# Loading the factors of both halves of an attention output ahead of its two multiplications

## The chip, the cores and the metric

The kernel runs on one core of one Trainium2 chip. The metric is the device time of one execution in microseconds (us), and a time is the median of several runs. A profile is of one execution; its times count from the start of that execution's span, and its engines are called PE (TensorE matmul), PEld (its weight loads), DVE (VectorE), ACT (ScalarE), POOL (GpSimd) and SP (SyncE, which here issues nearly all DMAs).

## The reference

One layer of a hybrid decoder block on a sequence of 1024 tokens with 1024 features, all in float32. After a conditioned RMSNorm and one input projection it has two branches, a gated DeltaNet (A) and a dilated sliding-window attention in three head groups of four heads (B), which are merged:

```python
o_b = jnp.stack(outs, axis=2)
w_g = jax.nn.softmax(jnp.stack(lses, axis=2), axis=2)
y_b = (o_b * w_g[..., None].astype(o_b.dtype)).reshape(b, s, ATTN_WIDTH) * jax.nn.silu(zb)
y_b = y_b @ w_proj_b[l]

merged = jax.nn.sigmoid(ga) * y_a + jax.nn.sigmoid(gb) * y_b
x = x + gate[:, None] * (merged @ w_out[l])
return rms_norm(x, final_norm_w)
```

The change is about the line with `w_g`: each head's attention output is multiplied by a weight for each token, here called its factor, and then by `silu(zb)`.

## The kernel before

Every tile has 128 partitions. Features lie on the partitions, and the 1024 tokens along the free dimension.

**How the order comes about.** The kernel is written as some hundred generators, called streams (`q_stream`, `ya_split`, `yb_split`, `tail_products` and so on). A planner (`Sched.run`) lets them take turns while the program is being built: it keeps an estimated clock for each engine, resumes the stream with the best priority whose waits have been met by those clocks, and records what the stream issues up to its next `yield`. Each engine then runs its instructions in exactly the recorded order, and waits on semaphores for what the data need. So an instruction that waits holds up everything behind it on its engine. That holds for SP too: a DMA whose target tile is still being read holds up all later DMAs.

Each DMA of SP also signals on one of eight semaphores in turn and waits, before it is issued, for the transfer eight places ahead of it.

**The tail of the program.** From about 1040 us on `tail_products` records, for PE, eight products A (here A product 0 to 7, `pa_units`, 8 x 6 matmuls each, weights `w_pa`), then eight products B (B product 0 to 7, `pb_units`, 6 x 6 matmuls each, weights `w_pb`), then the eight products with `w_out`. A product is a [128, 1024] tile in PSUM; the pool `pj` has two of these. For accuracy each float32 operand is split into a high part (a rounded copy, made by ACT) and a low part (the rest, made by DVE, or by POOL for `w_out`), and `three` records three matmuls for each operand pair, on two halves of 512 columns each: high by high, then high by the factor's low part, then the weights' low part. `YA[0..7]` are the split operands of the A products and `YB[0..5]` those of the B products. Every B product reads `YB[0]` to `YB[5]` in this order, so that B product 0 is the first reader of all six.

An output of an A product (`pa_out`) multiplies it on DVE with a gate tile that was loaded from DRAM (`gate_load`) and frees its place in `pj`; an output of a B product (`pb_out`) does the same, adds the A product's result, and splits the sum for the product with `w_out`.

**The six units.** `YB[j]` is made by `yb_split`, of which two copies run as streams; here its work on one j is called unit j. Unit j holds the two heads `2 * ti` and `2 * ti + 1` of group g (g = j // 2, ti = j % 2). It

1. takes two tiles of the pool `big` and loads the attention output `og` and the gate `z` into them (512 KB each, from `og_d[j]` and `z_d[8 + j]`),
2. multiplies `og` by its factors, 512 tokens at a time. The factors are rows of a small DRAM tensor `fg_d[g]`, written shortly before by `combine(g)`; two DMAs of 128 KB each spread a row over 64 partitions of a tile `fx` of the pool `mid` (six tiles of [128, 512]),
3. multiplies `z` by the result on DVE, with the tokens permuted for g = 1 and 2,
4. splits the product into `YB[j]` (ACT, then DVE).

The pool `big` has 34 tiles. Towards the end of the A products it is full, and the tiles for the last loads are those that A product 7 gives back, one factor of `YA` after another (`big.put(2)` in `tail_products`). The weights of each product come in through the pool `wr` (two tiles), are split into two tiles of `wh`, and the next load into `wr` waits for DVE's half of the split.

All instructions are issued through one helper (`Engine.call`), so the profile gives line 129 to nearly all of them, and one goes by tile names: `og` and `z` are `big`, `fx` is `mid`, `fg_d` is `fgd`, `og_d` is `ogd`, `z_d` is `zd`, and the gates are `gd`.

Of the kernel before, what the change touches and what calls it, by code (L numbers as in the profile page):

```python
# [10 lines left out]
OP = mybir.AluOpType  # L11
# [22 lines left out]
HALVES = (slice(0, 512), slice(512, 1024))  # L34
# [251 lines left out]
def hybrid_block_kernel(ctx: ExitStack, tc: tile.TileContext, x, c, norm_w, ada_w, ada_b, w_tiles, w_vb0, w_vb1,  # L286
# [3 lines left out]
    pe, act, dve, pool, sp = S.pe, S.act, S.dve, S.pool, S.sp  # L290
# [15 lines left out]
    mid = Slots(S, midp, "mid", 6, [P, 512])  # L306
# [624 lines left out]
    def perm(ap, g):  # L931
        if g == 0:
            return ap
        r = 4 if g == 1 else 8
        return ap.rearrange("p (u r) -> p r u", r=r)
# [836 lines left out]
    def split(dst, i, src, ev, slots=None, add=None, owed=0, eng=None):  # L1772
        hi = yield from (slots or big).get(F32R, add=add, owed=owed)
        lo = yield from (slots or big).get(F32R, add=add)
        act.activation(hi, src, AF.Copy)
        yield
        (eng or dve).tensor_tensor(lo, src, hi.bitcast(F32), op=OP.subtract)
        dst[i] = (hi, lo)
        S.set(ev)
# [27 lines left out]
    def yb_split():  # L1807
        yield ev_yas[7]
        while yb_todo:
            j = yb_todo.pop(0)  # L1810
            g, ti = j // 2, j % 2
            rows4 = fg_d[g].rearrange("(h i) p -> h (i p)", h=4)
            yield [ev_fg[g], ev_zd[8 + j]]
            yield lambda: len(big.free_at) > big.debt + 1
            og = yield from big.get()
            z = yield from big.get()
            sp.dma_start(og, og_d[j])
            sp.dma_start(z, z_d[8 + j])
            for q in range(2):
                sl = HALVES[q]  # L1820
                fx = yield from mid.get()
                for hd in range(2):
                    sp.dma_start(fx[64 * hd:64 * hd + 64, :],
                                 rows4[2 * ti + hd:2 * ti + hd + 1, sl].to_broadcast([64, 512]))
                yield
                dve.tensor_tensor(og[:, sl], fx, og[:, sl], op=OP.mult)
                mid.put()
            r = (1, 4, 8)[g]
            dve.tensor_tensor(perm(z, g), perm(z, g), og.rearrange("p (r u) -> p r u", r=r) if g else og, op=OP.mult)
            big.put()  # L1830
            yield
            yield from split(YB, j, z, ev_ybs[j], add=0)
            big.put()
# [217 lines left out]
    S.add(ya_split(), 8, "yas")  # L2051
    S.add(ya_split(), 8.1, "yas")
    S.add(yb_split(), 8, "ybs")
    S.add(yb_split(), 8, "ybs")
    S.add(wo_split(), 8, "wos")
    S.add(rows_stream(), 9, "rows")
# [68 lines left out]
```

## Time and profile before

| | us |
|---|---|
| median of 3 runs | 1280.1 (1279.59 to 1283.01) |
| the profiled execution | 1281.23 |
| its span, first to last instruction | 1279.5 |
| PE busy | 1252.6 |
| DVE busy | 766.2 |
| ACT busy | 502.2 |
| POOL busy | 173.6 |

The DMA engines moved 172.03 MB, 134 GB/s over the span. The mean granted clock of TensorE was 0.996 of full speed. In a timeline a row gives start, duration, engine, operation, the tile written and the tiles read, and in brackets the idle time of the engine ahead of it and what ended that. Busy time of an engine is an average over the span; where the time of a stage goes is read from the waits in that stage.

### The profile page before, as it was taken

Reading aid. Unit: us, or ns where it says so; the run is one execution under the profiler, and the core shown is the slowest. Engines: PE = TensorE matmul, PEld = TensorE weight load, DVE = VectorE, ACT = ScalarE, POOL = GpSimd, SP = SyncE. Lnnn points to the kernel's source line nnn. Section 1 sums busy time; section 2 is a strip of 40 time slices with the busy share of each in tenths; the row PEclk is TensorE's granted clock in tenths of the full one; section 3 lists DMA queues with packets and bytes.
Section 4 is the critical chain, followed back from the end, with each engine's and each line's share of the span. In section 5 each row is a group of like instructions: output and inputs, shape, how many; then the busy total and the mean of one; then the engine's idle time right before and its main releaser. Section 6 shows DMA issues by size and latency. Waiting matters only on the chain.

```text
span 1279.5 us, 19222 instructions
## 1 busy us (share of the span) xinstructions
PE 1252.6 (98%) x7302; PEld 1029.3 (80%) x7302; DVE 766.2 (60%) x1528; ACT 502.2 (39%) x1081; POOL 173.6 (14%) x128
## 2 busy tenths in 40 slices
PE   7999999999999999999999999999999999999997
PEld 3689888988888978888888888887777678778786
DVE  5845893457874368864669834555555546655533
ACT  5524622346223345233462335335555842122211
POOL 4700300033001022000320002300000000002400
PEclk9999999999999999999999999999999999999999
DMA  9534433153422262332343223635454857843322
GB/s 356 199 111 146 120 92 88 67 155 114 112 75 75 78 203 76 98 107 77 107 118 111 74 76 91 227 136 153 141 155 143 270 166 229 267 135 110 143 95 83
DMA packets 112558, 172.03 MB, mean 134 GB/s; under 512 B 41009, under 2 KB 72913, under 8 KB 112466
## 3 DMA queue, kind: packets, MB, share of 16 engines
q1 hardware_dynamic: 112322, 170.55, 42.5%
q8 instruction: 57, 0.93, 0.3%
q14 instruction: 35, 0.29, 0.1%
q10 hardware_dynamic: 144, 0.26, 0.1%
HBM read 123.40 MB, written 47.37 MB: 133 GB/s over the span
## 4 chain that ended last, share of the span: by engine, by line
PE 80%; DMA 5%; DVE 5%; issue 4%; ACT 3%; POOL 2%; SPq 0%; POOLq 0%; DVEq 0%; ACTq 0%
PE pj L129 60%; PE sb L129 20%; DVE big L129 3%; DMA big<-in_x_dram 2%; ACT big L129 1%; DMA wr<-in_w_out_dram 1%; DMA big<-grow 1%; POOL big L129 1%; POOL wh L129 1%; DVE wh L129 1%; ACT L129 1%; DVE mid L129 1%; ACT wh L129 0%; DMA mid<-yad 0%; SPq L129 0%
## 5 line engine op out<-in xcount | busy, mean ns | idle before, releaser
L129 PE MATMUL pj<-big,wh 128*128 128x512 f32 x3356 | 827.1, 398 | 4.5 <-DVE big L129 2.3
L129 PEld LDWEIGHTS pj<-big,wh 128*128 128x128 f32 x3356 | 616.3, 188 | 135.8 <-issue 8.9
L129 ACT ACTIVATE wh<-wr 128x1024 fp32r<-128x1024 f32 (+3 forms) x99 | 97.4, 984 | 242.3 <-PE pj L129 221.7
L129 DVE TENSOR_TENSOR wh<-wr,wh 128x1024 fp32r<-128x1024 f32 (+3 forms) x96 | 115.4, 1202 | 64.9 <-ACT wh L129 64.5
L129 ACT ACTIVATE big<-big 128x1024 f32<-128x1024 f32 (+2 forms) x77 | 74.1, 969 | 185.8 <-DVE big L129 137.3
L129 PE MATMUL pj<-wh,big 128*128 128x256 f32 (+2 forms) x702 | 110.7, 308 | 0.5 <-POOL wh L129 0.3
L129 PE MATMUL sb<-big,wh 128*128 128x512 f32 x368 | 103.4, 421 | 0.0
L129 PEld LDWEIGHTS pj<-wh,big 128*128 128x128 f32 x702 | 96.2, 189 | 6.5 <-POOL wh L129 0.7
L129 DVE SCALAR_TENSOR_TENSOR big<-pj,cw,big 128x1023 f32<-128x1023 f32 (+2 forms) x72 | 92.1, 1279 | 1.7
L129 PEld LDWEIGHTS sb<-big,wh 128*128 128x128 f32 x368 | 67.2, 190 | 20.6 <-issue 8.1
L129 DVE TENSOR_TENSOR big<-big,big 128x1024 f32<-128x1024 f32 (+4 forms) x44 | 58.1, 1326 | 21.6 <-ACT big L129 19.4
L129 PE MATMUL sb<-sq,big 128*128 128x128 f32 x464 | 67.1, 276 | 3.0 <-ACT sq L129 2.2
L129 PEld LDWEIGHTS sb<-sq,big 128*128 128x128 f32 x464 | 62.6, 191 | 8.9 <-ACT sq L129 3.1
L129 POOL TENSOR_TENSOR wh<-wr,wh 128x1024 fp32r<-128x1024 f32 x3 | 9.1, 3048 | 350.5 <-ACT wh L129 350.5
L129 ACT ACTIVATE big<-sb 128x512 f32<-128x512 f32 (+2 forms) x80 | 40.9, 523 | 35.6 <-PE sb L129 35.5
L129 DVE SCALAR_TENSOR_TENSOR sq<-sq,gsm,sb 128x128 f32<-128x128 f32 x48 | 16.6, 345 | 62.9 <-PE sb L129 61.7
L129 PEld LDWEIGHTS sb<-cst,big 128*128 128x128 f32 x268 | 33.9, 145 | 23.8 <-DVE big L129 8.2
L129 PE MATMUL sb<-cst,big 128*128 128x128 f32 x268 | 44.1, 285 | 7.8 <-DVE rstd L129 4.9
L129 PE MATMUL pj<-big,big 128*128 128x512 f32 x210 | 49.3, 390 | 0.0
L129 ACT ACTIVATE mid<-sb 128x512 f32<-128x512 f32 (+3 forms) x48 | 24.0, 501 | 63.7 <-PE sb L129 63.3
L129 ACT ACTIVATE big<-big,sta 128x128 f32<-128x128 f32 (+1 forms) x96 | 42.2, 442 | 13.0 <-DVE sta L129 12.9
L129 DVE CUSTOM_DVE_ANT_0 big<-sb,cst 128x128 f32<-128x128 f32 (+1 forms) x96 | 28.9, 347 | 29.0 <-PE sb L129 26.2
(140 smaller groups left out, 1282.5 us busy)
## 6 DMA issues: line engine op xcount, KB each, us to landing
wr<-in_w_tiles_dram SPq DMA_DIRECT2D x64, 512.0 KB, 4.2
big<-in_ada_w_dram SPq DMA_DIRECT2D x24, 512.0 KB, 9.0
big<-in_x_dram SPq DMA_DIRECT2D x16, 512.0 KB, 5.5
gd<-big SPq DMA_DIRECT2D x16, 512.0 KB, 2.9
big<-gd SPq DMA_DIRECT2D x16, 512.0 KB, 5.4
big<-grow SPq DMA_DIRECT2D x8, 512.0 KB, 5.7
vtd<-big SPq DMA_DIRECT2D x8, 512.0 KB, 2.6
big<-vtd SPq DMA_DIRECT2D x32, 128.0 KB, 5.0
```

The lines of the kernel that those rows point to most:

```text
L129: r = f(*a, **k)
```

## The change

In `yb_split` the two tiles for the factors are taken together, and all four factor DMAs are issued ahead of the multiplications. Before, each half had its own tile, its two DMAs, a `yield`, its multiplication, and gave its tile back.

```diff
             sp.dma_start(og, og_d[j])
             sp.dma_start(z, z_d[8 + j])
+            fx = yield from mid.many(2)
             for q in range(2):
-                sl = HALVES[q]
-                fx = yield from mid.get()
                 for hd in range(2):
-                    sp.dma_start(fx[64 * hd:64 * hd + 64, :],
-                                 rows4[2 * ti + hd:2 * ti + hd + 1, sl].to_broadcast([64, 512]))
-                yield
-                dve.tensor_tensor(og[:, sl], fx, og[:, sl], op=OP.mult)
-                mid.put()
+                    sp.dma_start(fx[q][64 * hd:64 * hd + 64, :],
+                                 rows4[2 * ti + hd:2 * ti + hd + 1, HALVES[q]].to_broadcast([64, 512]))
+            yield
+            for q in range(2):
+                dve.tensor_tensor(og[:, HALVES[q]], fx[q], og[:, HALVES[q]], op=OP.mult)
+            mid.put(2)
             r = (1, 4, 8)[g]
             dve.tensor_tensor(perm(z, g), perm(z, g), og.rearrange("p (r u) -> p r u", r=r) if g else og, op=OP.mult)
```

`many(n)` waits until n tiles of the pool are free and takes them one after the other. Since the planner now has one turn of these streams fewer between the loads and the product with z, it records other instructions in between. The instructions of PE and of POOL stand as before, apart from the buffers that they use; SP, DVE and ACT have the same instructions in another order within the units' stretch.

On SP, the end of the units' loads stood so before. `ogd4` and `zd12` belong to unit 4, `ogd5` and `zd13` to unit 5, `fgd2` are their factors (x2 is the pair of DMAs of one half); `gd7` is the gate of A product 7, `gd8` that of B product 0, `in_w_pb` the weights of a B product:

```order
L129 DMA big251_9691<-gd7_135 128x1024
L129 DMA big252_9703<-ogd4_190 128x1024
L129 DMA big253_9706<-zd12_172 128x1024
L129 DMA mid152_9709<-fgd2_195 64x512 x2
L129 DMA wr85_9730<-in_w_pb_dram 128x768
L129 DMA big256_9735<-ogd5_191 128x1024
L129 DMA big257_9736<-zd13_173 128x1024
L129 DMA mid153_9739<-fgd2_195 64x512 x2
L129 DMA mid154_9757<-fgd2_195 64x512 x2
L129 DMA big258_9772<-gd8_136 128x1024
L129 DMA mid155_9791<-fgd2_195 64x512 x2
```

Here the second half of unit 4 (`mid154`) comes after all of unit 5's first loads, and the second half of unit 5 (`mid155`) after gate 8. Now, at the same place on SP:

```order
L129 DMA big251_9640<-ogd4_190 128x1024
L129 DMA big252_9641<-zd12_172 128x1024
L129 DMA mid152_9644<-fgd2_195 64x512 x2
L129 DMA mid153_9645<-fgd2_195 64x512 x2
L129 DMA wr84_9668<-in_w_pb_dram 128x768
L129 DMA big255_9714<-gd7_135 128x1024
L129 DMA big256_9723<-ogd5_191 128x1024
L129 DMA big257_9724<-zd13_173 128x1024
L129 DMA mid154_9727<-fgd2_195 64x512 x2
L129 DMA mid155_9728<-fgd2_195 64x512 x2
L129 DMA wr85_9746<-in_w_pb_dram 128x768
L129 DMA big260_9784<-gd8_136 128x1024
```

Unit 4's loads have moved together, ahead of gate 7, and unit 5's ahead of gate 8. In the order before, `zd12` goes into the tile of the low part of `YA[0]`, `ogd5` and `gd8` into later tiles of A product 7's factors; now `gd7` goes into the tile of the low part of `YA[0]`, `ogd5` into that of its high part and `zd13` into that of the low part of `YA[1]`.

On DVE, from the output of A product 7 (the first row, which reads `pj79`) to that of B product 0 (the last, `pj80`), before. Rows that read a `mid` multiply half an attention output by its factors, rows of 128x8x128 are products with z, rows that write a `wh` make the low part of weights, and the other rows with 128x1024 make the low part of a unit:

```order
L129 SCALAR_TENSOR_TENSOR big251_9691<-big251_9691,pj79_9693 128x1024
L129 TENSOR_TENSOR wh193_9776<-wr84_9642,wh192_9775 128x768
L129 TENSOR_TENSOR big256_9735<-mid153_9739,big256_9735 128x512
L129 TENSOR_TENSOR big252_9703<-mid154_9757,big252_9703 128x512
L129 TENSOR_TENSOR big253_9706<-big253_9706,big252_9703 128x8x128
L129 TENSOR_TENSOR big256_9735<-mid155_9791,big256_9735 128x512
L129 TENSOR_TENSOR big257_9736<-big257_9736,big256_9735 128x8x128
L129 TENSOR_TENSOR big260_9813<-big253_9706,big259_9812 128x1024
L129 TENSOR_TENSOR big262_9819<-big257_9736,big261_9818 128x1024
L129 SCALAR_TENSOR_TENSOR big258_9772<-big258_9772,pj80_9774 128x1024
```

The low part of unit 4 (`big260`) stands behind the second half of unit 5 (`mid155`) and its product with z. Now, from the output of A product 6 (the first row, `pj78`) to that of B product 0:

```order
L129 SCALAR_TENSOR_TENSOR big250_9630<-big250_9630,pj78_9632 128x1024
L129 TENSOR_TENSOR big254_9706<-big247_9579,big253_9682 128x1024
L129 TENSOR_TENSOR wh191_9709<-wr83_9592,wh190_9708 128x768
L129 TENSOR_TENSOR big259_9740<-big252_9641,big258_9739 128x1024
L129 TENSOR_TENSOR big256_9723<-mid154_9727,big256_9723 128x512
L129 TENSOR_TENSOR big256_9723<-mid155_9728,big256_9723 128x512
L129 TENSOR_TENSOR big257_9724<-big257_9724,big256_9723 128x8x128
L129 SCALAR_TENSOR_TENSOR big255_9714<-big255_9714,pj79_9716 128x1024
L129 TENSOR_TENSOR wh193_9788<-wr84_9668,wh192_9787 128x768
L129 TENSOR_TENSOR big262_9796<-big257_9724,big261_9795 128x1024
L129 SCALAR_TENSOR_TENSOR big260_9784<-big260_9784,pj80_9786 128x1024
```

The low part of unit 4 (`big259`) has moved ahead of all work on unit 5, and the output of A product 7 (`pj79`) behind unit 5's two multiplications and its product with z.

## The prediction

> **What bounds the kernel now.** I read the page first, then the waits of PE (TensorE), then the timelines of the engines around those waits.
>
> ```profile
> span 1279.5 us, 19222 instructions
> PE 1252.6 (98%) x7302; PEld 1029.3 (80%) x7302; DVE 766.2 (60%) x1528; ACT 502.2 (39%) x1081; POOL 173.6 (14%) x128
> ```
>
> PE is busy for 98% of the span, and the change leaves PE's own instructions and their order as they are. So it can save time only where PE stands still, and cost time only where PE newly stands still. The changed code runs from about 1063 us on. These are PE's waits from 1040 us to the end:
>
> ```profile
> PE pj L129 <- DVE big L129: 2.3, 1, 2.3
> PE pj L129 <- ACT big L129: 1.4, 1, 1.4
> PE pj L129 <- POOL wh L129: 0.3, 1, 0.3
> ```
>
> Three waits in 240 us. PE's timeline says where the first two are (the bracket is the idle time ahead and its releaser):
>
> ```profile
> 1068.37 49.69 PE L129 MATMUL pj<-big,wh 128*128 128x512 f32 x218
> 1119.48 0.73 PE L129 MATMUL pj<-big,wh 128*128 128x512 f32 x2 [1.42 <-ACT big L129]
> 1122.52 61.28 PE L129 MATMUL pj<-big,wh 128*128 128x512 f32 x262 [2.31 <-DVE big L129]
> ```
>
> Both lie in B product 0, the first that reads the factors' result. Now DVE (VectorE) there:
>
> ```profile
> 1102.00 1.25 DVE L129 SCALAR_TENSOR_TENSOR big<-big,pj 128x1024 f32<-128x1024 f32 x1
> ...
> 1107.55 0.69 DVE L129 TENSOR_TENSOR big<-mid,big 128x512 f32<-128x512 f32 x1 [1.16 <-DMA mid<-fgd]
> 1112.66 1.22 DVE L129 SCALAR_TENSOR_TENSOR big<-big,pj 128x1024 f32<-128x1024 f32 x1 [4.42 <-PE pj L129]
> 1113.80 0.95 DVE L129 TENSOR_TENSOR wh<-wr,wh 128x768 fp32r<-128x768 f32 x1
> 1114.66 1.49 DVE L129 TENSOR_TENSOR big<-mid,big 128x512 f32<-128x512 f32 x2
> 1116.19 2.15 DVE L129 TENSOR_TENSOR big<-big,big 128x1024 f32<-128x1024 f32 x1
> 1118.52 0.69 DVE L129 TENSOR_TENSOR big<-mid,big 128x512 f32<-128x512 f32 x1 [0.19 <-DMA mid<-fgd]
> 1119.25 4.43 DVE L129 TENSOR_TENSOR big<-big,big 128x1024 f32<-128x1024 f32 x3
> ...
> 1134.88 1.22 DVE L129 SCALAR_TENSOR_TENSOR big<-big,pj 128x1024 f32<-128x1024 f32 x1 [3.44 <-PE pj L129]
> ...
> 1143.04 1.22 DVE L129 SCALAR_TENSOR_TENSOR big<-big,pj 128x1024 f32<-128x1024 f32 x1 [3.33 <-PE pj L129]
> ```
>
> With the order of DVE's rows in hand this reads so. 1107.55 is unit 4's first half, 1112.66 the output of A product 7 (PE has just begun B product 0), 1114.66 the first half of unit 5 and the second of unit 4, 1116.19 unit 4's product with z. At 1118.52 comes unit 5's second half, held until its factors landed. The three from 1119.25 are unit 5's product with z, then the low part of unit 4, then that of unit 5. **Unit 4's low part thus stands behind unit 5's late factors**, and PE's 2.31 us is the wait for it. The 1.42 us before is the high part of unit 4, which ACT (ScalarE) could start only after 1118.3:
>
> ```profile
> 1118.37 1.06 ACT L129 ACTIVATE big<-big 128x1024 fp32r<-128x1024 f32 x1 [5.27 <-DVE big L129]
> ```
>
> The stop has a tail. In the windows of one us, the column behind POOL is the granted clock:
>
> ```profile
> 1123.00:1124.00 1.00, 1.00 (x5) 0.76 (x4) 0.68 (x1) 0.00 (x0) 0.00 (x0) 0.62 0.00 0
> 1124.00:1125.00 1.00, 1.00 (x4) 0.80 (x3) 0.00 (x0) 0.00 (x0) 0.00 (x0) 0.50 0.00 0
> 1125.00:1126.00 1.00, 1.00 (x4) 0.72 (x3) 0.00 (x0) 0.20 (x1) 0.00 (x0) 0.50 0.00 0
> 1126.00:1127.00 1.00, 1.00 (x5) 0.82 (x4) 0.39 (x1) 0.64 (x1) 0.00 (x0) 0.68 0.00 0
> ```
>
> Missing clock: 0.38 + 0.50 + 0.50 + 0.32 = 1.70 us of PE work. A check without the modelled ends: the outputs at 1112.66, 1134.88 and 1143.04 close A product 7, B product 1 and B product 2. A B product at full pace takes 1143.04 - 1134.88 = 8.16 us, so products 0 and 1 lost 22.22 - 2 x 8.16 = **5.90 us**, against 1.42 + 2.31 + 1.70 = 5.43 from the rows. I take 5.90; the 0.47 between them lies in matmul ends that are only modelled.
>
> **The change part by part.** No instruction is added or removed: 12 multiplications of about 0.69 us, 24 factor loads and the six products with z remain. Only their places move, and with them the waits that they stand behind.
>
> *Unit 4.* Today SP (SyncE, which issues these loads) works through its end in this order:
>
> ```profile
> 1093.02 0.34 SPq L129 DMA_DIRECT2D wr<-in_w_pb_dram  x1
> ...
> 1102.68 0.32 SPq L129 DMA_DIRECT2D big<-zd  x1
> ...
> 1105.29 0.34 SPq L129 DMA_DIRECT2D wr<-in_w_pb_dram  x1
> 1105.73 0.57 SPq L129 DMA_DIRECT2D big<-ogd  x1
> 1106.35 0.43 SPq L129 DMA_DIRECT2D big<-zd  x1
> 1106.83 2.67 SPq L129 DMA_DIRECT2D mid<-fgd  x4
> 1109.60 0.54 SPq L129 DMA_DIRECT2D big<-gd  x1
> 1110.18 1.25 SPq L129 DMA_DIRECT2D mid<-fgd  x2
> ```
>
> 1102.68 is unit 4's z, into a tile that A product 7 has to leave first; 1106.83 holds unit 4's second half, and 1110.18 unit 5's second, behind a gate load. In the changed order all six loads of unit 4 stand ahead of the first load that waits for A product 7, and its z goes into a tile of unit 2. Its last multiplication moves ahead of the output of A product 6 (1102.00), its low part ahead of unit 5's multiplications. PE wants it at 1112.66 + 4 x 1.36 = 1118.1 (1.36 is a sixth of 8.16). The cover is more than 10 us, so both stops at unit 4 go. What is late next is unit 5.
>
> *Unit 5.* Now gate load 7, unit 5's output tile and its z wait for A product 7, for the last reads of the first factor's low part, the first's high part and the second's low part. The first is the very release of 1102.68. The others follow two and six matmuls later, 0.45 and 1.36 us at that pace (36 matmuls in 8.16 us): 1103.1 and 1104.0. The z load takes 0.43 us to issue and each factor load 0.62 (1.25 for two), so the last factor load goes out at 1104.0 + 0.5 + 3 x 0.62 = 1106.4, against 1110.8 now. How long does it take to land? The first row is of the tiles that these eight loads of 1103.0 to 1111.0 fill, the second of all transfers from or to the factor rows, the third of the pair at 1110.18:
>
> ```profile
> DMA to landing us min/median/max: 3.6/6.6/7.7
> DMA to landing us min/median/max: 1.4/6.5/8.4
> mid<-fgd SPq DMA_DIRECT2D x2, 128.0 KB, 7.6
> ```
>
> It lands between 1110.0 (3.6) and 1114.8 (8.4); I take 6.6, so 1113.0, because gate 7, unit 5's tile and its z are in flight ahead of it, as in the rows around 1106. From there DVE has the second multiplication 0.73, the product with z 2.15, the output of A product 7 now behind it 1.14, a weight split 0.86 and the low part 1.14: 6.0 us (start to start from the rows above). Unit 5 is ready at 1119.0, at the ends 1116.0 and 1120.8. PE asks for it in the third matmul of the last sixth of B product 0: 1112.66 + 5 x 1.36 + 0.45 = 1119.9. So **nothing is left of the stop at the value I take, and 0.9 us at the far end**. Below nothing cannot come out, since PE keeps its pace ahead of this.
>
> *Output of A product 7.* It now stands on DVE behind unit 5's multiplications: the added wait. At 1113.0 it starts at 1115.9 in place of 1112.66. Queued behind it are the split of B product 2's weights and unit 5's low part, counted above. PE needs its PSUM tile again for B product 1 at 1112.66 + 8.16 = 1120.8: cover 3.7 us.
>
> *Units 0 to 3* cost nothing: PE runs 49.69 us without a stop beside them, and their results are read only after 1112.66.
>
> *After B product 0* everything hangs on PE. The chain of work that ended last has
>
> ```profile
> 1122.52 44.52 PE pj L129 x188
> 1167.04 0.03 ACTq L129
> ...
> 1201.44 59.69 PE pj L129 x262
> ```
>
> The split of the output weights that ends in the third wait (0.3 us at 1201.44) is started by PE itself at 1167.04. It moves forward with PE and stays as long.
>
> **Sum.** The profiled execution took 1281.23 us (span 1279.5, 1.7 around it): 1281.23 - 5.90 = **1275.3**. It lies 1.1 above the median of the runs, 1280.1; the same saving from the median would give 1274.2. I keep 1275.3, for a reason that is the first rival.
>
> **The rivals.**
>
> *1. The slow clock is not in every execution.* The rows show half clock for some 3.4 us after two stops of 1.42 and 2.31 us with two matmuls between, and none after the 0.28 at 1201. If the median execution had the stops and not the slow clock, the median would lose 5.90 - 1.70 = 4.20: 1280.1 - 4.2 = **1275.9**. For it speaks that the fastest run, 1279.59, lies 1.64 under the profiled one; against it, that no trace shows such a run. [...]
>
> *2. Part of the stop stays.* Unit 5's factors land at 8.4 us or a little more, since two more of them travel together: 0.9 to 2.5 us of wait remain, **1276.2 to 1277.8**. For it: the margin is only 0.9 us, and the landing of 7.6 at 1110.18. Against it: fewer bytes are in flight ahead than then.
>
> *3. The wait only moves.* Unit 5's last factors land after 1117 because the three big loads ahead of them crowd the transfers, as at 1110.18 where each took over 7 us. Then unit 5 is ready after 1123, PE stops for 3 to 4 us, and the slow clock returns: **1279 to 1281**. Against it: the issue lies 4.4 us earlier.
>
> *4. Slower: SP's queue slips.* Each load waits for the one issued eight places ahead, and the store of group 1's factors now stands behind two more pairs of factor loads. That store is slow already:
>
> ```profile
> fgd<-mid SPq DMA_DIRECT2D x3, 16.0 KB, 8.0
> ```
>
> If the delay adds up over units 0 to 4, gate load 7 no longer waits for PE but for SP. It decides only beyond 1102.68 - 1094.2 = 8.5 us of slip, where 1094.2 is the issue of B product 2's weights, just ahead of it (now at 1093.02; its buffer comes free 1.14 us later, by the low part of unit 2 that DVE now does before that split). It costs more than the stop did beyond 8.5 + 0.9 + 5.9 = 15.3 us, one for one: at 20 us, 1281.2 + 4.7 = **1286**. Against it: one more landing of 8.0 us is the most that I can find.
>
> That the change does not do what it says is out: the rows of the order show both factor pairs of each unit together.
>
> **How the numbers follow.** About 0.3%, 3.8 us here, is what a measurement can tell from no change; from 1280.1 the bounds are 1276.3 and 1283.9. Forecast (5.9 saved, 1275.3, own range 1274.2 to 1276.2): 0.50. Rival 1 (1275.9): 0.20. Rival 2: 0.14. Rival 3: 0.10. Rival 4: 0.06. Faster takes the forecast and nearly all of rival 1, 0.68; slower is rival 4, 0.06; the rest, 0.26, is the same. The range 1273.8 to 1278.6 holds the first three cases with half a us for the scatter: 0.82 or so.
>
> **What would show it.** Right: no PE wait on ACT or DVE between 1112 and 1125, a granted clock of 1.00 there, B products 8.16 us apart from the first, SP issuing the last factor load at about 1106.4, unit 5's low part done by 1119.9. If the output of A product 7 starts at 1115 to 1116, the DVE order is as read. Rival 2 shows as one PE wait below 2.5 us in the last sixth of B product 0, rival 3 as one of 3 to 4 us with half clock behind it, rival 4 as gate load 7 issued well after 1103. The prediction is wrong if PE's waits go and the time does not fall by 4 us, or if an A product comes to stop before 1112.

## The result and the profile after

| | before | after |
|---|---|---|
| median | 1283.01 us (13 runs, 1279.59 to 1285.82) | 1276.59 us (13 runs, 1272.92 to 1396.33) |
| ratio | | 0.9947, 95% interval 0.9931 to 0.9962 |

The changed kernel is faster by 0.53%, 6.8 us of 1283.01 (4.9 to 8.9 by the interval). The execution profiled with these runs was a disturbed one (1396.33 us at a granted clock of 0.85): the ratio leaves it out, the medians of the table do not and lie 6.4 us apart, and the profile shown is of the repetition that is told below as e1_after, of an execution that took 1277.98 us.

The head of the changed kernel's page, to be set beside 1279.5 and 1252.6 of before:

```profile
span 1276.2 us, 19231 instructions
PE 1251.3 (98%) x7302; PEld 1028.6 (81%) x7302; DVE 766.5 (60%) x1528; ACT 502.3 (39%) x1081; POOL 173.5 (14%) x128
```

PE has as many matmuls as before, and the nine instructions more (19222 before) are waits on semaphores (four more on SP, six on DVE, one fewer on ACT). PE's waits from 1040 us to the end, of the same kernel, and its timeline from the last A products on:

```profile
PE pj L129 <- POOL wh L129: 0.3, 1, 0.3
```

```profile
1071.03 109.53 PE L129 MATMUL pj<-big,wh 128*128 128x512 f32 x482
```

The waits for DVE and ACT are gone: one row of 482 matmuls runs through all of B product 0, where before had three rows with 1.42 and 2.31 us between them. The third wait, for the output weights, stays at 0.3 us.

Now DVE from the output of A product 6 to that of B product 2:

```profile
1107.69 1.23 DVE L129 SCALAR_TENSOR_TENSOR big<-big,pj 128x1024 f32<-128x1024 f32 x1
...
1114.58 0.69 DVE L129 TENSOR_TENSOR big<-mid,big 128x512 f32<-128x512 f32 x1 [2.53 <-DMA mid<-fgd]
1115.70 0.69 DVE L129 TENSOR_TENSOR big<-mid,big 128x512 f32<-128x512 f32 x1 [0.43 <-DMA mid<-fgd]
1116.43 2.16 DVE L129 TENSOR_TENSOR big<-big,big 128x1024 f32<-128x1024 f32 x1
1118.48 1.21 DVE L129 SCALAR_TENSOR_TENSOR big<-big,pj 128x1024 f32<-128x1024 f32 x1
1119.61 0.95 DVE L129 TENSOR_TENSOR wh<-wr,wh 128x768 fp32r<-128x768 f32 x1
1120.47 1.22 DVE L129 TENSOR_TENSOR big<-big,big 128x1024 fp32r<-128x1024 f32 x1
1123.47 1.22 DVE L129 SCALAR_TENSOR_TENSOR big<-big,pj 128x1024 f32<-128x1024 f32 x1 [1.78 <-PE pj L129]
...
1131.63 1.22 DVE L129 SCALAR_TENSOR_TENSOR big<-big,pj 128x1024 f32<-128x1024 f32 x1 [3.33 <-PE pj L129]
...
1139.79 1.22 DVE L129 SCALAR_TENSOR_TENSOR big<-big,pj 128x1024 f32<-128x1024 f32 x1 [3.33 <-PE pj L129]
```

Only unit 5 is left beside the end of A product 7: 1114.58 and 1115.70 are its two halves, each held for its factors. The output of A product 7 (1118.48) stands behind them, then the split of weights, then unit 5's low part at 1120.47. The outputs of B products 0, 1 and 2 follow at 1123.47, 1131.63 and 1139.79, 8.16 us apart from the first.

**A measure for the stop.** The stretch ahead does not end at the same time in every execution: A product 5's output, the last one ahead of all that moves, starts at 1093.61 here and at 1090.90 in the profile of before. So the stop is measured from that output to the output of B product 2. At PE's full pace these lie 2 x 10.88 + 3 x 8.16 = 46.24 us apart (10.88 is eight sixths of 1.36, an A product). What is over that is called **lost** below. The two kernels in the windows of this stretch, before first and after second; the second figure of a row is PE's busy time and the one ahead of the DMA share the granted clock:

```profile
1090.00:1143.00 53.00, 49.27 (x209) 39.99 (x208) 33.38 (x30) 10.96 (x12) 0.00 (x0) 0.97 0.67 202
```

```profile
1093.00:1140.00 47.00, 47.00 (x209) 38.93 (x208) 30.16 (x28) 11.04 (x12) 0.00 (x0) 1.00 0.70 214
```

As many matmuls, 209, take 53 us with 49.27 busy at a clock of 0.97 before, and 47 us, all of them busy at 1.00, after. By the outputs, before lost 1143.04 - 1090.90 - 46.24 = 5.90 us, and after 1139.79 - 1093.61 - 46.24 = -0.06, that is nothing. What comes behind is as long as it was: from B product 2's output to the span's end 1279.5 - 1143.04 = 136.5 us and 1276.2 - 1139.79 = 136.4.

### The profile page after: what moved, and what is told of

Read it like the earlier page. It is cut to its first block, busy times and chain, and to the rows that moved or that the text cites. A ratio compares the mean times of both kernels' runs of the same rounds, so it can differ in the third digit from the quotient of the medians.

```text
span 1394.6 us, 19231 instructions
## 1 busy us (share of the span) xinstructions
PE 1374.4 (99%) x7302; PEld 1074.6 (77%) x7302; DVE 766.5 (55%) x1528; ACT 502.8 (36%) x1081; POOL 171.1 (12%) x128
## 4 chain that ended last, share of the span: by engine, by line
PE 96%; ACT 2%; issue 1%; DMA 1%; DVE 1%; POOL 0%; SPq 0%; POOLq 0%; DVEq 0%; ACTq 0%
PE pj L129 72%; PE sb L129 23%; ACT big L129 1%; DMA mid<-yad 0%; DVE big L129 0%; ACT wh L129 0%; ACT L129 0%; ACT mid L129 0%; DMA big<-in_c_dram 0%; POOL big L129 0%; DVE sq L129 0%; DVE wh L129 0%; POOL rstd L129 0%; ACT junk L129 0%; ACT pj L129 0%
## 5 line engine op out<-in xcount | busy, mean ns | idle before, releaser
L129 PE MATMUL pj<-big,wh 128*128 128x512 f32 x3356 | 908.4, 426 | 0.0
L129 PEld LDWEIGHTS pj<-big,wh 128*128 128x128 f32 x3356 | 634.5, 194 | 186.5 <-issue 11.1
L129 PE MATMUL pj<-wh,big 128*128 128x256 f32 (+2 forms) x702 | 117.8, 321 | 0.0
L129 PE MATMUL sb<-big,wh 128*128 128x512 f32 x368 | 113.7, 452 | 0.0
L129 PEld LDWEIGHTS pj<-wh,big 128*128 128x128 f32 x702 | 101.5, 197 | 7.7
L129 PE MATMUL sb<-sq,big 128*128 128x128 f32 x464 | 74.8, 299 | 2.6 <-ACT sq L129 2.1
L129 PEld LDWEIGHTS sb<-sq,big 128*128 128x128 f32 x464 | 69.3, 205 | 9.9 <-ACT sq L129 2.9
L129 PE MATMUL pj<-big,big 128*128 128x512 f32 x210 | 54.2, 417 | 0.0
L129 DVE SCALAR_TENSOR_TENSOR big<-sb,s_all,big 128x128 f32<-128x128 f32 x128 | 35.2, 344 | 27.0 <-PE sb L129 20.1
L129 PEld LDWEIGHTS pj<-big,big 128*128 128x128 f32 x210 | 40.3, 192 | 12.4
```

The costliest lines, as they stand in the source:

```text
L129: r = f(*a, **k)
```

## The experiments

The theory is the prediction's: the gain is the time for which PE stands still in B product 0 with the slow clock behind it, and it is set by the moment at which the last multiplication of units 4 and 5 is through on DVE. Three rivals: the loading in pairs gains at every unit; what counts is that the two multiplications stand side by side; or the pair of the one late unit does it. The saving is 1 - ratio, times the median of before in the same rounds. The diffs are against the kernel before, and `...` stands for lines left out.

**e1_after.** The changed kernel again, without an edit.

> The changed kernel as it is, for a profile at the full clock. Theory (the stop): the saving is the stop of B product 0 alone, so PE shows no wait on ACT or DVE over 0.9 us between 1112 and 1125 us, the output of A product 7 starts at 1115 to 1116 us, the last factor load of unit 5 is issued near 1106.4 us, and the time is 5 to 7 us under the kernel before in the same rounds. Rival (clock): the stop is still there with 2 us or more, and the saving comes from stretches of half clock that these executions lack.

Measured: 1278.13 us against 1285.48, ratio 0.9943 (0.9922 to 0.9964), 7.3 us saved; nothing lost, as shown. SP at the place that matters:

```profile
1105.34 0.33 SPq L129 DMA_DIRECT2D big<-gd  x1
1105.79 0.35 SPq L129 DMA_DIRECT2D big<-ogd  x1
1106.69 0.32 SPq L129 DMA_DIRECT2D big<-zd  x1
1107.07 2.37 SPq L129 DMA_DIRECT2D mid<-fgd  x4
1110.95 0.34 SPq L129 DMA_DIRECT2D wr<-in_w_pb_dram  x1
```

Gate 7, unit 5's two tiles and its four factor loads go out together, ahead of the weights (`wr`), which can only go out at 1110.95, when the split of the weights before them on DVE is done (1109.95 + 0.97 = 1110.92).

**e8_before_again.** The kernel before, without an edit, for a second profile of it.

> The kernel before once more, for a second profile. Theory (the stop): the same two PE waits, together 3.5 to 4 us, at the same place. [...] Time equal to the kernel before.

Measured: 1283.73 us against 1284.81, ratio 1.0 (0.9984 to 1.0016). PE and the windows behind its stop:

```profile
1122.05 0.73 PE L129 MATMUL pj<-big,wh 128*128 128x512 f32 x2 [2.15 <-ACT big L129]
1124.98 40.40 PE L129 MATMUL pj<-big,wh 128*128 128x512 f32 x170 [2.20 <-DVE big L129]
```

```profile
1124.00:1125.00 1.00, 0.02 (x1) 0.02 (x1) 1.00 (x2) 0.89 (x1) 0.00 (x0) 0.98 0.00 0
1125.00:1126.00 1.00, 1.00 (x2) 0.81 (x3) 1.00 (x1) 0.00 (x0) 0.00 (x0) 0.50 0.00 0
```

The same two stops and the same half clock behind them, in another execution. Lost: 6.50 us, so the two profiles of before stand at 5.90 and 6.50, mean 6.2.

**e2_units45.** Pairs for units 4 and 5 alone; units 0 to 3 as before.

```diff
+            if j >= 4:
+                fx = yield from mid.many(2)
...
+                for q in range(2):
+                    dve.tensor_tensor(og[:, HALVES[q]], fx[q], og[:, HALVES[q]], op=OP.mult)
+                mid.put(2)
+            else:
...
```

> Both factor loads together for units 4 and 5 only; units 0 to 3 load one half at a time as before. Theory (the stop): only what PE waits for in B product 0 counts. Unit 4's low part is ahead of unit 5 on DVE again, and unit 5's last factor load goes out at about 1108.7 us (1110.8 before), so 0.5 to 1.5 us of the stop stay: 4 to 5.5 us saved. Rival (every unit counts): a third of the units gives a third of the saving, about 2 us.

Measured: 1281.74 us against 1285.48, ratio 0.997 (0.9953 to 0.9988), 3.9 us saved. PE keeps two short stops, and no half clock follows them:

```profile
1122.61 0.73 PE L129 MATMUL pj<-big,wh 128*128 128x512 f32 x2 [1.06 <-ACT big L129]
1123.87 41.33 PE L129 MATMUL pj<-big,wh 128*128 128x512 f32 x181 [0.53 <-DVE big L129]
```

Lost: 2.17. On DVE and SP it shows why unit 5 is late:

```profile
1107.68 0.96 DVE L129 TENSOR_TENSOR wh<-wr,wh 128x768 fp32r<-128x768 f32 x1
```

```profile
1108.67 0.34 SPq L129 DMA_DIRECT2D wr<-in_w_pb_dram  x1
1109.11 0.38 SPq L129 DMA_DIRECT2D big<-ogd  x1
1109.54 0.42 SPq L129 DMA_DIRECT2D big<-zd  x1
1110.13 2.37 SPq L129 DMA_DIRECT2D mid<-fgd  x4
```

The weights stand ahead of unit 5 on SP here. They wait for DVE's split, which ends at 1107.68 + 0.96 = 1108.64, and unit 5's loads, which do not need it, queue behind. In the changed kernel it is the other way round. So the late units' pairs alone do not end the whole stop: that takes the pairs of units 0 to 3 too, and by the rows it is the order which the planner then gives to unit 5.

**e3_units0to3.** The counterpart: pairs for units 0 to 3, units 4 and 5 as before.

```diff
+            if j < 4:
+                fx = yield from mid.many(2)
...
```

> Both factor loads together for units 0 to 3 only; units 4 and 5 load one half at a time as before. The planner reaches units 4 and 5 earlier, so that the low part of unit 4 stands ahead of all work on unit 5, and unit 5's last factor load goes out at about 1107 us, ahead of gate 8. Theory (the stop): unit 5 is ready at about 1119.8 us against 1119.9 wanted, so 0 to 1 us of the stop stays: 5 to 6 us saved. Rival (the pairs of units 4 and 5 are what helps): with these loaded one half at a time the stop stays whole, nothing saved. Rival (every unit counts): about 4 us.

Measured: 1281.07 us against 1285.48, ratio 0.9963 (0.9943 to 0.9982), 4.8 us saved. Waits of PE 1.04 and 0.53 us, no half clock, lost 2.09. Units 4 and 5 are loaded one half at a time here, and yet two thirds of the stop are gone. So most of the gain needs no pair at the late unit.

**e9_unit4_only and e10_unit5_only.** A pair for one unit alone (`j == 4`, and `j == 5`).

```diff
+            if j == 4:
+                fx = yield from mid.many(2)
...
```

> Both factor loads together for unit 4 alone. On DVE the low part of unit 4 then stands ahead of unit 5, but on SP the second half of unit 5 now stands behind gate 8 and behind the weights of B product 4, which wait for a split that DVE does after the output of A product 7. Theory (the stop): the stop at unit 4 goes, that at unit 5 grows to 4.5 to 6.5 us in one piece, with half clock behind it: 0 to 4 us slower than the kernel before. Rival (every unit counts): about 1 us saved. Rival (loading a pair together helps the unit that gets it): 2 to 3 us saved, the first of the two stops.

> Both factor loads together for unit 5 alone. On DVE the second half of unit 4 and its product with z now stand behind all of unit 5. Theory (the stop): PE still waits for unit 4, ready at 1122 to 1124 us against 1118.1 wanted (in the times of the profile before), 4 to 6 us of PE waits: from 1.5 us faster to 2 us slower than the kernel before. Rival (every unit counts): about 1 us saved. Rival (unit 5 is the late one, so its pair is the change): 4 to 7 us saved.

Measured, against 1286.57 us: 1287.71, ratio 1.0007 (0.9993 to 1.0021), and 1288.55, ratio 1.001 (0.9993 to 1.0026). Neither gains anything; in the profiles both lose more than before, 7.37 and 8.85 us. PE in the first, then in the second:

```profile
1132.48 32.76 PE L129 MATMUL pj<-big,wh 128*128 128x512 f32 x134 [4.98 <-ACT big L129]
```

```profile
1131.75 33.52 PE L129 MATMUL pj<-big,wh 128*128 128x512 f32 x135 [5.94 <-ACT big L129]
```

The two late places differ. SP in e9_unit4_only, behind unit 5's first pair of factor loads:

```profile
1116.22 1.09 SPq L129 DMA_DIRECT2D mid<-fgd  x2
1117.40 0.53 SPq L129 DMA_DIRECT2D big<-gd  x1
1123.10 0.34 SPq L129 DMA_DIRECT2D wr<-in_w_pb_dram  x1
1123.49 1.09 SPq L129 DMA_DIRECT2D mid<-fgd  x2
```

Unit 5's second half has slipped behind gate 8 and behind one more load of weights, which waits for a split (1122.13 + 0.94 = 1123.07) until 1123.10: 6 us later than it could go. DVE in e10_unit5_only:

```profile
1125.26 0.69 DVE L129 TENSOR_TENSOR big<-mid,big 128x512 f32<-128x512 f32 x1 [0.30 <-DMA mid<-fgd]
1125.99 2.00 DVE L129 TENSOR_TENSOR big<-big,big 128x1024 f32<-128x1024 f32 x1
1127.89 0.68 DVE L129 TENSOR_TENSOR big<-mid,big 128x512 f32<-128x512 f32 x1
```

Here unit 5's pair has overtaken unit 4: the row at 1127.89 is the second half of unit 4, which PE wants first, behind unit 5's second half and its product with z. So a pair is not worth a fixed sum for each unit. What it is worth depends on what it passes.

**e4_loads_together.** The loads of both halves together, but a turn of the planner ahead of each multiplication.

```diff
+            fx = yield from mid.many(2)
...
+            for q in range(2):
                 yield
-                dve.tensor_tensor(og[:, sl], fx, og[:, sl], op=OP.mult)
-                mid.put()
+                dve.tensor_tensor(og[:, HALVES[q]], fx[q], og[:, HALVES[q]], op=OP.mult)
+            mid.put(2)
```

> Both factor loads together in all units, but a turn of the planner ahead of each multiplication. On SP the weights of B product 3 now stand ahead of unit 5's loads, and on DVE the output of A product 7 ahead of unit 5's multiplications. Theory (the stop): unit 5's last factor load goes out at about 1109.7 us, unit 5 is ready at 1121 to 1122, so 1 to 2 us of the stop stay: 3.5 to 5 us saved. Rival (multiplications side by side are what helps): nothing saved, since they are taken one at a time.

Measured: 1279.52 us against 1285.48, ratio 0.9954 (0.9936 to 0.9971), 5.9 us saved. Waits of PE 1.69 and 0.53 us, no half clock, lost 2.74. In e2, e3 and e4 more of the stop stayed than expected: by PE's waits alone 1.59, 1.57 and 2.22 us, against 0.5 to 1.5, 0 to 1 and 1 to 2.

**e5_mults_together.** The counterpart: the multiplications side by side, the second half loaded a turn later than the first.

```diff
+            fx = yield from mid.many(2)
             for q in range(2):
...
+                if q:
+                    yield
                 for hd in range(2):
...
+            yield
+            for q in range(2):
+                dve.tensor_tensor(og[:, HALVES[q]], fx[q], og[:, HALVES[q]], op=OP.mult)
+            mid.put(2)
```

> The two multiplications side by side, but the second half's factors still loaded one turn later than the first's, so that on SP the second half of unit 4 stands behind all first loads of unit 5, and that of unit 5 behind gate 8, as before the change. Theory (the stop): unit 4's low part still stands behind unit 5's product with z, so the stop of B product 0 stays, 3 to 5 us of PE waits: within 1.5 us of the kernel before. Rival (multiplications side by side are what helps): 5 to 7 us saved.

Measured: 1285.43 us against 1284.81, ratio 1.0008 (0.9992 to 1.0023). PE waits longer than before:

```profile
1122.99 0.73 PE L129 MATMUL pj<-big,wh 128*128 128x512 f32 x2 [1.31 <-ACT big L129]
1126.32 38.99 PE L129 MATMUL pj<-big,wh 128*128 128x512 f32 x159 [2.59 <-DVE big L129]
```

Lost: 7.13. Of the two, it is the loads that carry most of the gain; the multiplications side by side have nothing by themselves. With the loads apart, the planner puts both multiplications of unit 4 behind the output of A product 7 on DVE, and everything of unit 5 behind them.

**e7_delayed and e11_delayed_more.** The changed kernel, with unit 5's output loaded twice, or four times, into the same tile, so that its factors go out later and all else stays.

```diff
             sp.dma_start(z, z_d[8 + j])
+            if j == 5:
+                sp.dma_start(og, og_d[j])
+            fx = yield from mid.many(2)
```

> The changed kernel with unit 5's attention output loaded twice into the same tile, the second load ahead of the four factor loads; it waits for the first one to land. Theory (the stop): unit 5's last factors land 4 to 6 us later, so PE waits 3.5 to 5.5 us in one piece in the last sixth of B product 0, and if half clock follows on such a stop another 1.7: 4 to 7 us lost against the changed kernel, within 1.5 us of the kernel before. Rival (clock or scatter, not the stop): as fast as the changed kernel.

> The changed kernel with unit 5's attention output loaded four times into the same tile, each load waiting for the one ahead, before the four factor loads. In the run with two loads the factors landed 2.4 us later than in the changed kernel and PE waited 1.29 us; two more loads add about 3.5 us each. Theory (the stop): one PE wait of 5.5 to 8 us in the last sixth of B product 0, with half clock behind it (no run showed half clock after waits of 0.5 to 2.2 us in all, each did after 3.7 to 4.4): 7 to 11 us slower than the changed kernel, 1 to 4 us slower than before. Rival (half clock needs two stops): 1.7 us less than that.

Measured: 1279.52 us against 1284.81, ratio 0.9961 (0.9946 to 0.9977), 5.0 saved, lost 1.92; and 1285.56 against 1286.57, ratio 0.9998 (0.9983 to 1.0014), nothing saved, lost 7.96. PE in the first, then PE and SP in the second:

```profile
1120.25 44.95 PE L129 MATMUL pj<-big,wh 128*128 128x512 f32 x197 [1.29 <-DVE big L129]
```

```profile
1126.03 39.24 PE L129 MATMUL pj<-big,wh 128*128 128x512 f32 x161 [5.26 <-ACT big L129]
```

```profile
1108.86 7.71 SPq L129 DMA_DIRECT2D big<-ogd  x3
1116.62 2.37 SPq L129 DMA_DIRECT2D mid<-fgd  x4
```

The direction is that of the theory, and both sizes were missed. One repeated load delayed the factors by far less than I had assumed (2.4 us against e1_after), so the first expectation, 4 to 7 us, was wrong: the dose was too small. With three repeats the wait came out at 5.26 us, just under the expected 5.5 to 8, and the time was that of before, not 1 to 4 us above it. In the first of these kernels the prediction's own step can be checked: factors used from t on make unit 5 ready at t + 6.0, wanted at 1119.9. With t = 1115.4 in the time of the profile before that is 1.5 us of wait, against 1.29.

**e6_turned.** The loads of before, but PE takes units 0 to 3 for B products 0 and 1 first, and units 4 and 5 for both after that, so that unit 4 is wanted four sixths of a product, 5.4 us, later.

```diff
-        for j in range(8):
+        pbt = {}
+        for j, ks in [(0, range(4)), (1, range(4)), (0, range(4, 6)), (1, range(4, 6))] + [(j, range(6)) for j in range(2, 8)]:
...
-            for kk in range(6):
+            for kk in ks:
```

> The kernel before with its loads as they were; only PE's order differs: B product 0 with units 0 to 3, B product 1 with units 0 to 3, then units 4 and 5 of both. PE asks for unit 4 at 1123.5 us of the profile before in place of 1118.1 and for unit 5 at 1124.9, and they are ready at 1122.5 and 1123.7. Theory (the stop): no wait is left, 5 to 6.5 us saved, as much as by the change. Rival (the loads' order itself, less waiting on SP or DVE): nothing saved, since SP, DVE and ACT do the same as before.

Measured: 1279.69 us against 1284.81, ratio 0.9954 (0.9939 to 0.997), 5.9 us saved. One wait is left:

```profile
1128.82 36.35 PE L129 MATMUL pj<-big,wh 128*128 128x512 f32 x159 [0.53 <-DVE big L129]
```

Lost: 0.84. Not one factor load is paired here. That most of the gain comes all the same shows that the pairs are worth only the stop which they end.

**e12_both.** The change and the turned order together.

```diff
+            fx = yield from mid.many(2)
...
+        for j, ks in [(0, range(4)), (1, range(4)), (0, range(4, 6)), (1, range(4, 6))] + [(j, range(6)) for j in range(2, 8)]:
```

> The change together with PE's turned order of B products 0 and 1. Theory (the stop): the change leaves no wait in B product 0, and the turned order left 0.5 us with the loads before; together no wait is left and the margin is 5 us wider, but nothing more can be saved: within 1 us of the changed kernel, 5 to 7 us under the kernel before. Rival (two separate savings): 10 to 13 us under the kernel before.

Measured: 1279.69 us against 1286.57, ratio 0.9946 (0.9925 to 0.9967), 6.9 us saved; lost -0.05. No more than the change alone (0.9943 and 0.9947): with the stop gone, nothing is left there for a second remedy.

**All of them together.** "Late" is the start of the last multiplication of units 4 and 5 on DVE, counted from PE's start of B product 0 (A product 5's output + 21.76). "By the trace" is 6.2, the mean of before, less the time lost. The two kernels in which PE runs another order have no place in the column "late".

| kernel | late, us | PE's waits, us | half clock, us | lost, us | saved by the trace | saved, measured (95%) |
|---|---|---|---|---|---|---|
| e1_after | 0.33 | none | 0 | -0.06 | 6.3 | 7.3 (4.6 to 10.0) |
| e7_delayed | 2.78 | 1.29 | 0 | 1.92 | 4.3 | 5.0 (3.0 to 6.9) |
| e3_units0to3 | 3.70 | 1.04 + 0.53 | 0 | 2.09 | 4.1 | 4.8 (2.3 to 7.3) |
| e2_units45 | 3.8 | 1.06 + 0.53 | 0 | 2.17 | 4.0 | 3.9 (1.5 to 6.0) |
| e4_loads_together | 4.40 | 1.69 + 0.53 | 0 | 2.74 | 3.5 | 5.9 (3.7 to 8.2) |
| before | 5.86 | 1.42 + 2.31 | 3.4 | 5.90 | | |
| e5_mults_together | 6.1 | 1.31 + 2.59 | 6.8 | 7.13 | -0.9 | -1.0 (-3.0 to 1.0) |
| e8_before_again | 6.50 | 2.15 + 2.20 | 3.4 | 6.50 | | 0.0 (-2.1 to 2.1) |
| e10_unit5_only | 7.48 | 5.94 | 6.8 | 8.85 | -2.6 | -1.3 (-3.3 to 0.9) |
| e9_unit4_only | 7.88 | 4.98 | 6.8 | 7.37 | -1.2 | -0.9 (-2.7 to 0.9) |
| e11_delayed_more | 8.10 | 5.26 | 6.8 | 7.96 | -1.8 | 0.3 (-1.8 to 2.2) |
| e6_turned | | 0.53 | 0 | 0.84 | 5.4 | 5.9 (3.9 to 7.8) |
| e12_both | | none | 0 | -0.05 | 6.2 | 6.9 (4.3 to 9.7) |

The later the last multiplication, the more is lost, nearly row by row, whatever edit made it late. And the time lost at this one place gives the measured saving within the interval for every kernel but e4_loads_together, where it is 0.2 us short of the lower end, and e11_delayed_more lies right at its lower end; each has one profile only. No saving outside this stretch is needed. Saving at every unit would fit e2 and e3; it falls by e6, which has most of the saving without a pair, and narrowly by e9 and e10, whose intervals end at 0.9 us where that rival asks for about 1. The side by side multiplications fall by e5, the one late pair by e3, e9 and e10.

The time lost also adds up from its parts. In each of the eleven profiles with a stop it is PE's waits, and half of the half-clock time in which PE was at work, and 0.3 to 0.6 us more. In e9_unit4_only, for example, PE stood still for 2.78 of the 6.83 us of half clock: 4.98 + 4.05 / 2 = 7.0, and 7.37 were lost. What the rest of 0.3 to 0.6 us is stays open; it comes with every stop, with or without half clock.

## Why the prediction came out right

To set its times beside e1_after, 2.71 us (1093.61 - 1090.90) are taken off the latter.

- **The stop.** 5.90 us were to go, and in the trace they went. Measured were 6.8 us (4.9 to 8.9). The term lies within that, but it came from one profile of before, and the other lost 6.50, so it is known to about 0.6 us.
- **Unit 4.** Both stops at unit 4 went, as forecast. Its low part was through at 1109.3, wanted at 1118.1: the cover was 8.8 us, not more than 10.
- **Unit 5's loads.** Gate 7 was to be released at 1102.68 and was issued at 1105.34 - 2.71 = 1102.63; the z load at 1103.98, forecast 1104.0; the last factor load at about 1106.1, forecast 1106.4.
- **Landing and what follows.** Forecast 1113.0 for the factors: the second multiplication starts at 1112.99. Output of A product 7: 1115.77, forecast 1115.9. Unit 5's low part is done at about 1118.9, forecast 1119.0, wanted at 1119.9. The margin of one microsecond is real, and e7_delayed shows it used up: its factors came 2.4 us later, and PE waited 1.29 us.
- **The added wait.** A product 7's output 3.1 us later in that frame (1112.66 before) stopped nothing, as its cover of 3.7 us said.
- **Rival 1**, the slow clock in only some executions, falls: both profiles of before have it, 3.4 us of half clock in each, and the 4.20 us that it left to save lie below the measured interval.
- **Rivals 2 and 3**, a part of the stop stays or it only moves, are not in the changed kernel, but their neighbours e7_delayed (1.29 us) and e11_delayed_more (5.26 us, and half clock) show that both were real possibilities. A stop like that of rival 3 does eat the gain: e11_delayed_more, with a longer one than it was priced for (3 to 4 us), saves nothing.
- **Rival 4**, a slip of SP's queue, falls with gate 7's issue: it is still PE that releases it.
- **The forecast as a time**, 1275.3, is 1.3 us under the median, which lies in the stated range of 1273.8 to 1278.6 but 0.4 above the forecast's own, 1274.2 to 1276.2. Its base was 1281.23, and before has since shown a median of 1283.01; 1283.01 - 5.90 = 1277.1 would have been 0.5 too high. The two errors, base and saving, partly cancel, and that is luck.

One thing the prediction did not see, and it mattered. I took A product 7's tiles as what holds unit 5's loads. In the order before there is also the load of weights ahead of them, which waits for a split on DVE (1105.29 in the rows of the prediction). In the changed kernel it has passed behind unit 5. e2 to e4 keep it in front, and each keeps 2.1 to 2.7 us of the stop. No run moved that load alone, so how much of the 2.1 to 2.7 us is its share is read from the rows, not measured.

## What to carry to other kernels

Read the engine that stops, then find what stands ahead of the late operand in each in-order queue on its way; here that was DVE's order and a load in SP's queue that waited (in e2_units45 until 1108.67 us) for something the late operand did not need. The same edit can be worth everything or less than nothing, depending on what it passes, so show the order on every queue before pricing it. Once the stop is gone, further remedies for it gain nothing, so stop there and look for the next wait.

## What the chip showed that was not expected

**Half clock followed on some stops and not on others.** The trace records the granted clock. In the profile of before it is 0.50 for 3.41 us from 48.03 us and again from 1123.23 us, and 1.00 from 51.45 to 1123.22 and from 1126.65 to 1276.8. In the windows around the stop of that profile (the second figure of a row is again PE's busy time)

```profile
1116.41:1119.82 3.41, 1.99 (x10) 1.33 (x8) 3.19 (x3) 1.06 (x1) 0.00 (x0) 1.00 0.86 273
1119.82:1123.23 3.41, 1.10 (x5) 0.63 (x4) 3.41 (x3) 1.06 (x1) 0.00 (x0) 1.00 0.01 4
1123.23:1126.65 3.42, 3.42 (x10) 2.64 (x9) 0.49 (x2) 0.84 (x1) 0.00 (x0) 0.50 0.00 0
```

PE stands still for 1.42 us of the first and 2.31 of the second, and half clock comes behind the second. Of the thirteen profiles of the table six have half clock beside the stop: both of before, e5, e9, e10 and e11. In these PE stood still for 2.20 us (e9_unit4_only) to 3.41 us (e10_unit5_only) of the 3.41 us ahead of half clock, and half clock began 2.2 us (e9_unit4_only) to 5.2 us (before) after the stop's start. The longest wait in each of the six is 2.20 us or more, and the waits add up to 3.73 us or more. In the other seven the longest wait is 1.69 us, and the waits add up to 2.22 us at most, both in e4_loads_together. So these profiles do not part the length of one wait from the sum of several, and they do not show why half clock comes. They do show that standstill alone does not tell it: in the 3.41 us ahead of 48.03 us in the profile of before PE is busy for 3.18, and half clock follows all the same.

Beside the stop half clock lasted 3.4 us in both profiles of before, where PE worked through it (0.03 us of standstill at most), and 6.8 us in e5, e9, e10 and e11, where PE stood still for the first 1.16 to 2.78 us of it.

**The same stretch does not take the same time.** PE's order is the same in all these kernels up to the B products, and yet A product 5's output started between 1089.60 us (e4_loads_together) and 1098.98 us (e9_unit4_only). The two kernels' windows from 100 to 200 us show a good part of that, e4_loads_together first:

```profile
100.00:200.00 100.00, 100.00 (x545) 85.98 (x545) 72.79 (x164) 41.81 (x80) 14.84 (x9) 1.00 0.37 114
```

```profile
100.00:200.00 100.00, 96.68 (x515) 82.57 (x515) 69.27 (x152) 41.78 (x79) 12.74 (x7) 0.97 0.38 113
```

PE is busy for 3.3 us less there in e9_unit4_only, at a clock of 0.97, and has done 30 matmuls fewer; its waits ahead of 1085 us hold one that e4_loads_together does not have:

```profile
PE sb L129 <- DVE qpart L129: 3.0, 1, 3.0
```

From 400 to 500 us the granted clock of e9_unit4_only is 0.98; that of e4_loads_together is 1.00 in both stretches. So a stop of PE and a slow clock come and go early in the program too, with nothing changed there. The whole scatter, 9.4 us, is more than the effect of the change. Two profiles are therefore compared between two outputs, and not by their times from the start.
